# Quarters of x and of two weight chunks multiplied together, and the last norm's work divided anew

## The chip, the cores and the metric

The kernel runs on one core of a Trainium2 chip. The metric is device microseconds of one execution; three runs of the kernel before gave a median of 1205.68 us (1205.36 to 1205.92). Engines are called by the names of the profile: PE (TensorE), DVE (VectorE), ACT (ScalarE), POOL (GpSimd), SP (SyncE, which here only issues transfers).

## What is computed

An encoder trunk of two layers on x of 256 tokens by 1024 channels, all in fp32. Each layer adds half a gated feed-forward, then three token mixers that share one input projection, then half a second feed-forward; a root-mean-square norm closes the trunk. The change touches the first feed-forward of the first layer and the last norm:

```python
def rmsnorm(x, g):
    r = lax.rsqrt(jnp.mean(xf * xf, axis=-1, keepdims=True) + EPS)
    return (xf * r * g.astype(jnp.float32)).astype(x.dtype)

def swiglu(h, w_in, w_out):
    g, u = jnp.split(h @ w_in, 2, axis=-1)
    return (jax.nn.silu(g) * u) @ w_out

x = x + 0.5 * swiglu(rmsnorm(x, norm_ffn1[l]), w_ffn1_in[l], w_ffn1_out[l])   # first step of a layer
...
return rmsnorm(x, norm_final)                                                  # the end
```

## The kernel before

**Precision by halves.** Each fp32 operand is split into a rounded part (hi, made by an ACT cast) and the remainder (lo, a subtraction on DVE, L307), and each product is three PE products: hi with hi, hi with lo, lo with hi (`mm3`, L323 to L325).

**Weights** come in chunks of 1 MB, [128, 8, 256] or [128, 2, 1024], through three raw buffers (`wraw`); `ahead` keeps loads five chunks and splits three chunks in front of their use. SP issues these loads one after the other; a load waits until its buffer is free. In what follows chunk 0 and chunk 1 are the first gate and up chunk of w_ffn1_in, chunk 2 and 3 the next gate and up chunk, and the chunk after 3 is the first of w_ffn1_out.

**The feed-forward** (`ffn`) goes over 11 pairs of gate and up chunks. For a pair, 48 products make the gate sums and 48 the up sums (8 K tiles, 2 halves, 3 products). Norm and projection commute: x is scaled by the norm's gain alone (xgh, xgl), and the factor r of each token is applied after the product, by R, which PE spreads over the partitions from a diagonal dg (L372). Then DVE gr = gate x R (L481), ACT silu (L482), POOL gr x R (L483), DVE hid (L503), ACT hh (L509), POOL hl (L510), and the products with w_out, one pair later (`outp`).

**The start** (L1003 to L1040): x comes as two halves of 128 tokens into a raw buffer; PE runs a few products on ones (`warm`), transposes x (ps_x), ACT and DVE make xgh and xgl of two K tiles at a time, and between them ACT and POOL split chunk 0, loaded in four quarters. xT, the squares of x and the sum sst follow, while PE multiplies chunk 0; chunk 1 is loaded and split whole after that.

**The end**: the last output products (`tokacc`) leave token-major sums for two token tiles (tt), in four quarters q each. `evac_tok` adds them to x on DVE and squares them on ACT; DVE multiplies the low 512 channels (LO) by the gain nf, sums and scales the squares, POOL raises them to -0.5, and both token tiles are scaled at the very end (`scale_out`), LO on ACT and the high half (HI) on DVE.

**Order.** PE's order is the order of the code throughout. Blocks marked BY_HAND also keep ACT's and DVE's instructions of that block in the code's order among themselves; all else on ACT, DVE, POOL and SP is placed by a scheduler at build time, which may put instructions of later code between those of a block.

Of the kernel before, what the change touches and what calls it, by code (L numbers as in the profile page):

```python
# [70 lines left out]
def encoder(ctx: ExitStack, tc: tile.TileContext, a, rope, onehot, out):  # L71
# [210 lines left out]
    specs[0] = ([((slice(None), slice(2 * i, 2 * i + 2)), specs[0][0][0][1][:, 2 * i:2 * i + 2]) for i in range(4)],) + specs[0][1:]  # L282
    raws, parts = [], []

    def ahead(n_raw, n_split):
        while len(raws) < min(n_raw, len(specs)):
# [6 lines left out]
            for _ in split(2):  # L293
                pass

    def split(n, eng=None):

        _, shape = specs[len(parts)]
        raw = raws[len(parts)]
        hi = whi.tile([P] + shape, F32R, tag="hi", name="hi")  # L300
        lo = wlo.tile([P] + shape, F32R, tag="lo", name="lo")
        parts.append((hi, lo))
        n = shape[0] // n
        for i in range(0, shape[0], n):
            h = slice(i, i + n)
            nc.scalar.copy(out=hi[:, h], in_=raw[:, h])  # L306
            (eng or nc.vector).tensor_sub(lo[:, h], raw[:, h], f(hi[:, h]))  # L307
            yield

    used = [0]  # L310
# [102 lines left out]
    BY_HAND = {mybir.EngineType.PE, mybir.EngineType.Activation, mybir.EngineType.DVE}  # L413
    late = []

    def ffn(gnext, final=False):
        accs = [bank(acc, "facc") for _ in range(4)]
        if final:
            fl = [x.rearrange("p a s -> p (a s)") for x in accs]
            accs = [fl[0:2], fl[2:4]]  # L420
            xt = [p4.tile([P, D], F32, tag="t4", name="xt") for _ in range(2)]
            fin = [p4.tile([P, D], F32, tag="t4", name="fin") for _ in range(2)]
            nf = p4.tile([P, D], F32, tag="t4", name="nf")
            ss = [sm.tile([P, 4], F32, name="ss") for _ in range(2)]
# [15 lines left out]
        r_fin = [sm.tile([P, 1], F32, name="r_fin") for _ in range(2)] if final else []  # L440

        def evac_tok(tt, q, ps):

            sl = slice(q * 256, (q + 1) * 256)
            nc.vector.scalar_tensor_tensor(out=fin[tt][:, sl], in0=ps, scalar=0.5, in1=xt[tt][:, sl], op0=ALU.mult, op1=ALU.add)
            nc.scalar.activation(out=t1("junk"), in_=fin[tt][:, sl], func=AF.Square, accum_out=ss[tt][:, q:q + 1])
            if (tt, q) == (0, 2):
                gain_lo(0)
            elif (tt, q) == (1, 1):
                rms(0)  # L450
            elif (tt, q) == (1, 3):
                gain_lo(1)
                rms(1)
                scale_out(0)
                scale_out(1)

        def gain_lo(tt):
            nc.vector.tensor_mul(fin[tt][:, LO], fin[tt][:, LO], nf[:, LO])

        def rms(tt):  # L460
            r = r_fin[tt]
            nc.vector.reduce_sum(out=r, in_=ss[tt], axis=AX.X)
            nc.vector.tensor_scalar(out=r, in0=r, scalar1=1.0 / D, scalar2=EPS, op0=ALU.mult, op1=ALU.add)
            nc.gpsimd.tensor_tensor(out=r, in0=r, in1=mhalf[:, 0:1], op=ALU.pow)

        def scale_out(tt):
            nc.scalar.mul(out=fin[tt][:, LO], in_=fin[tt][:, LO], mul=r_fin[tt])
            nc.vector.scalar_tensor_tensor(out=fin[tt][:, HI], in0=fin[tt][:, HI], scalar=r_fin[tt], in1=nf[:, HI], op0=ALU.mult, op1=ALU.mult)
# [17 lines left out]
        pend = None  # L486
        for j in range(NPAIR):
            w, ps = weights(), bank(wk, "gu")
            if j == 0:
                project_first(ps, w)  # L490
                stats_tok()
            else:
                project(ps, w, 0)
                project(ps, w, 1)
                gr = silu(ps)
            w, pu = weights(), bank(wk, "gu")
            project(pu, w, 0)
            if j == 0:
                stats_bcast()
                gr = silu(ps)  # L500
            project(pu, w, 1)
# [499 lines left out]


    ctx.enter_context(tc.manual_schedule(engines={mybir.EngineType.PE}))  # L1003
    ahead(2, 0)
    with tc.manual_schedule(engines=BY_HAND):

        hot = bank(wk, "hot")

        def warm(n):
            for _ in range(n):  # L1010
                nc.tensor.matmul(hot[:, 0, :P], lhsT=ones, rhs=ones, start=True, stop=True)

        warm(6)
        gains(rows, 2 * KT, 0)
        sst = sm.tile([P, 2], F32, name="sst", bufs=1)
        state["sst1"] = sm.tile([P, 2], F32, name="sst1", bufs=1)
        xps = [bank(acc, "ps_x") for _ in range(4)]
        for tt in range(2):
            for m in range(KT):
                nc.tensor.transpose(xps[m // 2][:, m % 2, cs(tt)], xtok[:, tt, cs(m)], ident)  # L1020
            warm(4)
        first = split(4, nc.gpsimd)
        for b in range(4):
            for i in range(2):
                m = 2 * b + i
                nc.scalar.activation(out=xgh[:, m, :], in_=xps[b][:, i, :], func=AF.Identity, scale=gcol[:, m:m + 1])
            for i in range(2):
                scaled_lo(2 * b + i, 0, xps[b][:, i, :])
            next(first)
        for _ in first:  # L1030
            pass
        for b in range(4):
            nc.vector.tensor_copy(out=xT[:, 2 * b:2 * b + 2, :], in_=xps[b])
        for tt in range(2):
            for i in range(2):
                junk = t2("junk").rearrange("p a s -> p (a s)")
                acc_to = sst if i == 0 else state["sst1"]
                nc.scalar.activation(out=junk, in_=xtok[:, tt, i * 512:(i + 1) * 512], func=AF.Square, accum_out=acc_to[:, tt:tt + 1])
        nc.vector.tensor_add(sst, sst, state["sst1"])
        state["sst"] = sst  # L1040
    for l in range(DEPTH):
        ffn(16 + KT * l)
        mixer(l)
        ffn(KT if l == 0 else None, final=(l == DEPTH - 1))

# [31 lines left out]
```

## Time and profile before

| | |
|---|---|
| median of three runs | 1205.68 us |
| the profiled execution | 1204.95 us, span 1203.2 us |
| PE busy | 1176.7 us, 98% of the span, 9748 products |
| DVE, ACT, POOL busy | 850.5, 678.6, 256.8 us |
| moved by DMA | 218.15 MB, mean 181 GB/s |
| mean granted clock of PE | 0.995 |

The span is the time from the first to the last instruction of the profiled execution. Busy PE means that products follow each other without a gap; a busy share of another engine tells nothing of the end unless PE waits for it. The granted clock is the share of PE's full 2.4 GHz that it was allowed; 0.50 is 1.2 GHz.

### The profile page before, as it was taken

To read this page: it belongs to the slowest core of one execution; us is meant where nothing else is said; L and a number is where in the kernel's file an instruction comes from. 1 tells how busy PE (TensorE), PEld (TensorE's weight loads), DVE (VectorE), ACT (ScalarE), POOL (GpSimd) and SP (SyncE) were. 2 spreads that over 40 slices of the span, in tenths; PEclk is the share of its full clock that TensorE was granted. 3 is DMA by queue.
4 is the path that set the end of the run, shared out by engine and by line. 5 is a ranking of instruction groups with operands and counts; after the bars stand their busy time and mean duration, and the time that the engine had idled before them with its cause. 6 is when DMAs were issued, how large, how long until landed. Compare 5 with 4: busy or idle time off the path is not lost.

```text
span 1203.2 us, 23180 instructions
## 1 busy us (share of the span) xinstructions
PE 1176.7 (98%) x9748; PEld 1150.1 (96%) x9748; DVE 850.5 (71%) x1145; ACT 678.6 (56%) x1117; POOL 256.8 (21%) x188
## 2 busy tenths in 40 slices
PE   8999999999999999999999999999998999999997
PEld 8999999998989999999999999998988999999996
DVE  5766668878887776666685656697787868656664
ACT  6444346579876554444454444466998566443443
POOL 2222224300021032121241212241000302212221
PEclk9999999999999999999999999999999999999999
DMA  7759665453545556565555565545443546565550
GB/s 255 257 179 309 205 209 176 141 175 118 172 136 181 176 180 206 181 206 192 195 175 192 194 207 180 192 158 176 141 162 120 174 141 198 193 203 180 193 192 35
DMA packets 169364, 218.15 MB, mean 181 GB/s; under 512 B 4302, under 2 KB 147200, under 8 KB 169260
## 3 DMA queue, kind: packets, MB, share of 16 engines
q1 hardware_dynamic: 168652, 215.09, 54.5%
q8 instruction: 76, 1.25, 0.4%
q10 hardware_dynamic: 464, 1.06, 0.2%
q0 software_dynamic: 144, 0.52, 0.1%
q14 instruction: 28, 0.23, 0.1%
HBM read 215.59 MB, written 4.22 MB: 183 GB/s over the span
## 4 chain that ended last, share of the span: by engine, by line
PE 75%; ACT 11%; DVE 9%; issue 3%; POOL 1%; DMA 0%; POOLq 0%; ACTq 0%
PE gu L324 13%; PE gu L323 13%; PE gu L325 13%; PE facc L323 5%; PE facc L325 5%; PE facc L324 5%; ACT hi L306 3%; DVE lo L307 3%; PE fm L324 2%; PE fm L323 2%; PE fm L325 2%; ACT e L625 2%; PE facc L407 2%; PE facc L406 2%; PE facc L405 2%
## 5 line engine op out<-in xcount | busy, mean ns | idle before, releaser
L307 DVE TENSOR_TENSOR lo<-raw,hi 128x1024 fp32r<-128x1024 f32 x390 | 539.5, 1397 | 138.2 <-ACT hi L306 137.4
L306 ACT CAST hi<-raw 128x1024 fp32r<-128x1024 f32 (+1 forms) x394 | 404.0, 1044 | 405.7 <-issue 352.8
L325 PE MATMUL gu<-xgh,lo 128*128 128x256 f32 x1408 | 389.4, 277 | 1.6 <-POOL lo L307 0.8
L323 PE MATMUL gu<-xgh,hi 128*128 128x256 f32 x1408 | 390.7, 277 | 0.3 <-ACT hi L306 0.3
L324 PE MATMUL gu<-xgl,hi 128*128 128x256 f32 x1408 | 390.1, 277 | 0.3 <-DVE xgl L338 0.3
L325 PEld LDWEIGHTS gu<-xgh,lo 128*128 128x128 f32 x1408 | 264.5, 188 | 2.2 <-POOL lo L307 1.1
L324 PEld LDWEIGHTS gu<-xgl,hi 128*128 128x128 f32 x1408 | 264.5, 188 | 1.8 <-DVE xgl L338 0.7
L323 PEld LDWEIGHTS gu<-xgh,hi 128*128 128x128 f32 x1408 | 264.3, 188 | 1.8 <-ACT hi L306 1.3
L323 PE MATMUL fm<-xgh,hi 128*128 128x256 f32 x640 | 179.7, 281 | 0.0
L324 PE MATMUL fm<-xgl,hi 128*128 128x256 f32 x640 | 178.8, 279 | 0.0
L325 PE MATMUL fm<-xgh,lo 128*128 128x256 f32 x640 | 178.3, 279 | 0.0
L483 POOL TENSOR_TENSOR gr<-gr,R 128x512 f32<-128x512 f32 x44 | 76.9, 1747 | 365.3 <-ACT gr L482 365.3
L325 PEld LDWEIGHTS fm<-xgh,lo 128*128 128x128 f32 x640 | 121.1, 189 | 0.0
L324 PEld LDWEIGHTS fm<-xgl,hi 128*128 128x128 f32 x640 | 120.4, 188 | 0.8
L323 PEld LDWEIGHTS fm<-xgh,hi 128*128 128x128 f32 x640 | 120.2, 188 | 0.1
L323 PE MATMUL facc<-hh,hi 128*128 128x256 f32 x384 | 106.0, 276 | 0.0
L324 PE MATMUL facc<-hl,hi 128*128 128x256 f32 x384 | 106.0, 276 | 0.0
L325 PE MATMUL facc<-hh,lo 128*128 128x256 f32 x384 | 106.0, 276 | 0.0
L510 POOL TENSOR_TENSOR hl<-hid,hh 128x512 fp32r<-128x512 f32 x35 | 62.5, 1787 | 123.7 <-ACT hh L509 123.7
L481 DVE TENSOR_TENSOR gr<-gu,R 128x512 f32<-128x512 f32 x44 | 30.4, 691 | 74.0 <-PE gu L325 73.8
L324 PEld LDWEIGHTS facc<-hl,hi 128*128 128x128 f32 x384 | 72.1, 188 | 0.0
L323 PEld LDWEIGHTS facc<-hh,hi 128*128 128x128 f32 x384 | 72.1, 188 | 0.0
(234 smaller groups left out, 1949.7 us busy)
## 6 DMA issues: line engine op xcount, KB each, us to landing
raw<-in_w_ffn_in_dram SPq DMA_DIRECT2D x87, 1024.0 KB, 5.1
raw<-in_w_ffn_out_dram SPq DMA_DIRECT2D x44, 1024.0 KB, 4.9
raw<-in_w_in_dram SPq DMA_DIRECT2D x38, 1024.0 KB, 5.1
raw<-in_w_branch_dram SPq DMA_DIRECT2D x12, 1024.0 KB, 5.2
raw<-in_w_out_dram SPq DMA_DIRECT2D x8, 1024.0 KB, 4.9
G<-skew SPq DMA_DIRECT2D x24, 192.0 KB, 5.0
raw<-in_w_in_dram SPq DMA_DIRECT2D x8, 512.0 KB, 4.8
skew<-vec_d SPq DMA_DIRECT2D x6, 512.0 KB, 8.7
```

Source lines behind the costliest of these rows:

```text
L306: nc.scalar.copy(out=hi[:, h], in_=raw[:, h])
L307: (eng or nc.vector).tensor_sub(lo[:, h], raw[:, h], f(hi[:, h]))
L323: nc.tensor.matmul(ps, lhsT=hi[:, k, sl], rhs=xh, start=st, stop=False, **chk)
L324: nc.tensor.matmul(ps, lhsT=hi[:, k, sl], rhs=xl, start=False, stop=False, **chk)
L325: nc.tensor.matmul(ps, lhsT=lo[:, k, sl], rhs=xh, start=False, stop=last, **chk)
L405: nc.tensor.matmul(ps, lhsT=xh[:, k, cs(tt)], rhs=w[0][:, k, sl], start=(first and k == 0), stop=False)
L406: nc.tensor.matmul(ps, lhsT=xh[:, k, cs(tt)], rhs=w[1][:, k, sl], start=False, stop=False)
L407: nc.tensor.matmul(ps, lhsT=xl[:, k, cs(tt)], rhs=w[0][:, k, sl], start=False, stop=(last and k == 1))
L481: nc.vector.tensor_mul(gr, ps, Rb)
L483: nc.gpsimd.tensor_mul(gr, gr, Rb)
L510: nc.gpsimd.tensor_sub(hl, hid, f(hh))
L625: nc.scalar.activation(out=e[:, qt, :], in_=e[:, qt, :], func=AF.Identity, scale=su[:, qt:qt + 1])
```

## The change

x goes into two [128, 2, 512] tiles of another pool and comes in four quarters of 256 channels (two K tiles) each, for all 256 tokens. Chunks 0 and 1 come in quarters of two K tiles too, the three kinds in turn, two of the quarters on ACT's queue and the rest on SP's. For each quarter PE transposes its two K tiles, ACT and DVE make xgh and xgl, and split the quarter of chunk 0 and of chunk 1 (DVE takes the lo of chunk 0 that POOL made); PE multiplies the quarter with chunk 0, transposes the next quarter, and multiplies with chunk 1. The first pair thus enters `ffn` as `begun`, and its R, silu and hid follow in the middle of chunk 2. ACT loads its table early, by an activation on mhalf. In the last norm nf is scaled once by sqrt(D); the LO product moves from DVE to POOL, the squares of a tile's last quarter from ACT to DVE, the sums become single additions, and each token tile is scaled and stored as soon as its own sums are there.

The diff, cut to its core:

```diff
+    xtok = [p4.tile([P, 2, D // 2], F32, tag="t4", name="xtok") for _ in range(2)]
+    raws = [wraw.tile([P, KT, 2 * P], F32, tag="raw", name="raw") for _ in range(2)]
+    for q in range(4):
+        nc.sync.dma_start(out=xtok[q // 2][:, :, 256 * (q % 2):256 * (q % 2 + 1)], in_=xv[:, :, 256 * q:256 * (q + 1)])
+        for i, raw in enumerate(raws):
+            src = a["w_ffn1_in"][0, 256 * q:256 * (q + 1), i * D_FF:i * D_FF + 2 * P]
+            (nc.scalar if i == 0 and q < 2 else nc.sync).dma_start(out=raw[:, 2 * q:2 * q + 2, :], in_=src.rearrange("(k p) n -> p k n", p=P))
...
-            nc.scalar.activation(out=t1("junk"), in_=fin[tt][:, sl], func=AF.Square, accum_out=ss[tt][:, q:q + 1])
-            if (tt, q) == (0, 2):
-                gain_lo(0)
...
-                scale_out(1)
+            if q < 3:
+                nc.scalar.activation(out=t1("junk"), in_=fin[tt][:, sl], func=AF.Square, accum_out=ss[tt][:, q:q + 1])
+            else:
+                nc.vector.tensor_tensor_reduce(out=t1("junk"), in0=fin[tt][:, sl], in1=fin[tt][:, sl], scale=1.0, scalar=ss[tt][:, 0:1], op0=ALU.mult, op1=ALU.add, accum_out=ss[tt][:, 3:4])
+                rms(tt)
+            if q == 1:
+                nc.gpsimd.tensor_mul(fin[tt][:, LO], fin[tt][:, LO], nf[:, LO])
+                nc.vector.tensor_scalar(out=ss[tt][:, 0:1], in0=ss[tt][:, 0:1], scalar1=ss[tt][:, 1:2], scalar2=EPS * D, op0=ALU.add, op1=ALU.add)
...
+                project(ps, w, 0)
+                if begun:
+                    stats_bcast()
+                    pend = hidden(0, begun[1], silu(begun[0]))
+                    begun = None
+                project(ps, w, 1)
...
+        splits = [split(4) for _ in range(2)]
         for b in range(4):
...
+            for c in range(2):
+                next(splits[c])
+                for m in (2 * b, 2 * b + 1):
+                    for t in range(2):
+                        mm3(begun[c][:, t, :], parts[c], m, cs(t), xgh[:, m, :], xgl[:, m, :], False, m == KT - 1, start=(m == 0 and t == 0))
+                if c == 0 and b < 3:
+                    turn(b + 1)
```

The scheduler's part of the change shows in the order of the instructions. ACT's queue at the start, in the kernel before; raw_139 is chunk 0, raw_144 chunk 1, raw_232 chunk 2, and hi_192, hi_238, hi_244 are their rounded parts:

```order
L1026 ACTIVATE xgh_129<-ps_x_160,gcol_131 128x256
L306 CAST hi_192<-raw_139 128x512 [waits DMAHW3_49]
L1026 ACTIVATE xgh_129<-ps_x_161,gcol_131 128x256 [waits PE_49]
L1026 ACTIVATE xgh_129<-ps_x_161,gcol_131 128x256
L306 CAST hi_192<-raw_139 128x512 [waits DMAHW4_49]
```

And now, where raw_105 is chunk 0, raw_106 chunk 1 and raw_363 chunk 2:

```order
L1044 ACTIVATE xgh_142<-ps_x_155,gcol_144 128x256
L309 CAST hi_189<-raw_105 128x512 [waits DMAHW2_49]
L309 CAST hi_209<-raw_106 128x512 [waits DMAHW3_49]
L309 CAST hi_373<-raw_363 128x1024 [waits DMAHW5_49]
L309 CAST hi_373<-raw_363 128x1024
L1044 ACTIVATE xgh_142<-ps_x_156,gcol_144 128x256 [waits PE_49]
L1044 ACTIVATE xgh_142<-ps_x_156,gcol_144 128x256
L309 CAST hi_189<-raw_105 128x512 [waits DMAHW4_49]
L309 CAST hi_209<-raw_106 128x512 [waits DMAHW6_49]
```

Both casts of chunk 2, which stood behind all of chunk 0, chunk 1 and the squares, now stand between quarter 0 and quarter 1; DVE's two subtractions for chunk 2 stand at the same place in its queue. SP's load of chunk 2 stands behind all the quarters of x and of chunks 0 and 1.

DVE's queue behind the last quarter, now (before, the copies of xT stood ahead of the sum sst):

```order
L1064 TENSOR_TENSOR sst_329<-sst_329,sst1_330 128x2 [waits Activation_49]
L1066 COPY xT_141<-ps_x_155 128x512
L1066 COPY xT_141<-ps_x_156 128x512
L1066 COPY xT_141<-ps_x_157 128x512
L1066 COPY xT_141<-ps_x_158 128x512
L358 TENSOR_SCALAR v_tok_349<-sst_329 128x2 [waits DVE_49]
L310 TENSOR_TENSOR lo_380<-raw_365,hi_379 128x1024 [waits DMAHW1_49,PE_49,Activation_49]
L362 TENSOR_SCALAR dg_353<-ident_96,r_tok_350 128x128 [waits Pool_49]
```

The copies of xT have moved between the sum and v, and so ahead of dg.

DVE's queue at the end, now; fin_12111 is token tile 0, fin_12112 token tile 1 (before, the scaling of both tiles' HI half stood last):

```order
L449 SCALAR_TENSOR_TENSOR fin_12111<-facc_12106,xt_12109 128x256
L453 ISA junk_13858,ss_12114<-fin_12111,ss_12114 128x256 [waits DVE_49]
L453 ISA ss_12114 128x1
L462 TENSOR_TENSOR ss_12114<-ss_12114 128x1 [waits DVE_49,Activation_49]
L465 SCALAR_TENSOR_TENSOR fin_12111<-fin_12111,ss_12114,nf_12113 128x512 [waits Pool_49]
L449 SCALAR_TENSOR_TENSOR fin_12112<-facc_12107,xt_12110 128x256 [waits PE_49]
```

Tile 0's scaling, which waits for POOL, now stands ahead of tile 1's first evacuation. On POOL the order is tile 0's LO product, tile 0's power, tile 1's LO product, tile 1's power.

## Rows read from the trace of the kernel before

**Rows 1.** Busy times by stage: stretch, length, busy time (count) by engine, clock, DMA, GB/s.

```profile
9.45:10.50 1.05, 0.58 (x4) 0.58 (x5) 0.72 (x2) 1.05 (x4) 1.05 (x2) 1.00 1.09 345
20.00:25.00 5.00, 5.00 (x42) 4.84 (x41) 3.07 (x4) 3.19 (x4) 0.00 (x0) 1.00 0.82 297
1198.00:1199.00 1.00, 0.00 (x0) 0.00 (x0) 0.55 (x2) 0.44 (x1) 0.53 (x1) 1.00 0.42 156
1199.00:1200.00 1.00, 0.00 (x0) 0.00 (x0) 0.31 (x1) 0.28 (x1) 0.00 (x0) 0.50 0.98 367
```

**Rows 2.** Timeline of PE: start, duration, engine, line, operation, tiles, count, idle before.

```profile
1.05 2.93 PE L1011 MATMUL hot<-ones 128*128 128x128 f32 x12 [1.05 <-DVE ind L143]
5.42 1.06 PE L1011 MATMUL hot<-ones 128*128 128x128 f32 x8
6.70 1.09 PE L1020 MATMUL ps_x<-ident,xtok 128*128 128x128 f32 x8 [0.22 <-DMA xtok<-in_x_dram]
19.59 0.59 PE L372 MATMUL halves<-dg,ones 128*128 128x256 f32 x2
22.85 0.28 PE L323 MATMUL gu<-xgh,hi 128*128 128x256 f32 x1
34.35 0.28 PE L323 MATMUL facc<-hp,hi 128*128 128x256 f32 x1
```

**Rows 3.** Timeline of ACT at the start.

```profile
8.41 0.85 ACT L1026 ACTIVATE xgh<-ps_x,gcol 128x256 fp32r<-128x256 f32 x2
9.13 0.63 ACT L306 CAST hi<-raw 128x512 fp32r<-128x512 f32 x1
20.82 2.00 ACT L306 CAST hi<-raw 128x1024 fp32r<-128x1024 f32 x2 [4.22 <-DMA raw<-in_w_ffn_in_dram]
25.83 1.28 ACT L482 ACT_TABLE_LOAD   x1
27.12 0.63 ACT L482 ACTIVATE gr<-gr 128x512 f32<-128x512 f32 x1
```

**Rows 4.** The chain that ended last, at ACT's squares of x: start, duration, piece.

```profile
12.27 2.45 ACT junk L1038 x8
```

**Rows 5.** Timeline of DVE at the start.

```profile
9.29 0.87 DVE L338 SCALAR_TENSOR_TENSOR xgl<-ps_x,gcol,xgh 128x256 fp32r<-128x256 f32 x2 [0.37 <-ACT xgh L1026]
12.59 2.47 DVE L1033 COPY xT<-ps_x 128x512 f32<-128x512 f32 x4
15.69 2.36 DVE L307 TENSOR_TENSOR lo<-raw,hi 128x1024 fp32r<-128x1024 f32 x2 [0.36 <-ACT hi L306]
17.97 0.48 DVE L359 TENSOR_SCALAR dg<-ident,r_tok 128x128 f32<-128x128 f32 x2
24.18 0.42 DVE L374 COPY R<-halves 128x256 f32<-128x256 f32 x1
24.63 0.69 DVE L481 TENSOR_TENSOR gr<-gu,R 128x512 f32<-128x512 f32 x1
```

**Rows 6.** DMA issues of the first 4 us: tensor, queue, count, size, median us to landing.

```profile
raw<-in_w_ffn_in_dram SPq DMA_DIRECT2D x1, 1024.0 KB, 8.4
```

**Rows 7.** Timeline of SP's queue at the start: issue of chunk 0's quarters and chunk 1.

```profile
1.19 2.81 SPq L290 DMA_DIRECT2D raw<-in_w_ffn_in_dram  x5
```

**Rows 8.** Timeline of POOL at the start.

```profile
15.41 0.71 POOL L356 TENSOR_TENSOR r_tok<-v_tok,mhalf 128x2 f32<-128x2 f32 x1 [1.76 <-DVE v_tok L355]
27.83 1.30 POOL L483 TENSOR_TENSOR gr<-gr,R 128x512 f32<-128x512 f32 x1 [11.71 <-ACT gr L482]
```

**Rows 9.** Timeline of ACT, POOL and DVE in the last 12 us.

```profile
1192.71 0.19 ACT L446 ACTIVATION_READ_ACCUMULATOR junk<-fin 128x1 f32 x1
1195.36 0.55 POOL L464 TENSOR_TENSOR r_fin<-r_fin,mhalf 128x1 f32<-128x1 f32 x1 [7.92 <-DVE r_fin L463]
1197.53 0.99 POOL L464 TENSOR_TENSOR r_fin<-r_fin,mhalf 128x1 f32<-128x1 f32 x1 [1.62 <-DVE r_fin L463]
1198.56 0.75 DVE L468 SCALAR_TENSOR_TENSOR fin<-fin,r_fin,nf 128x512 f32<-128x512 f32 x1 [0.45 <-POOL r_fin L464]
```

More of the change, by code (lines that the diff above doesn't have):

```diff
@@ L280, in encoder @@
         specs += ffn_chunks(a["w_ffn2_in"][l], a["w_ffn2_out"][l])
-    specs[0] = ([((slice(None), slice(2 * i, 2 * i + 2)), specs[0][0][0][1][:, 2 * i:2 * i + 2]) for i in range(4)],) + specs[0][1:]
-    raws, parts = [], []
+    parts = []
     def ahead(n_raw, n_split):
@@ L294, in ahead, with split @@
                 pass
-    def split(n, eng=None):
+    def split(n):
         _, shape = specs[len(parts)]
@@ L306, in split @@
             nc.scalar.copy(out=hi[:, h], in_=raw[:, h])
-            (eng or nc.vector).tensor_sub(lo[:, h], raw[:, h], f(hi[:, h]))
+            nc.vector.tensor_sub(lo[:, h], raw[:, h], f(hi[:, h]))
             yield
@@ L414, in encoder, with ffn @@
     late = []
-    def ffn(gnext, final=False):
+    def ffn(gnext, final=False, begun=None):
         accs = [bank(acc, "facc") for _ in range(4)]
@@ L425, in ffn @@
             nc.gpsimd.dma_start(out=nf, in_=a["norm_final"].partition_broadcast(P))
+            nc.gpsimd.tensor_scalar_mul(nf, nf, math.sqrt(D))
         def back(tt):
@@ L439, in ffn @@
         LO, HI = slice(0, 512), slice(512, 1024)
-        r_fin = [sm.tile([P, 1], F32, name="r_fin") for _ in range(2)] if final else []
         def evac_tok(tt, q, ps):
@@ L445, in evac_tok @@
             nc.vector.scalar_tensor_tensor(out=fin[tt][:, sl], in0=ps, scalar=0.5, in1=xt[tt][:, sl], op0=ALU.mult, op1=ALU.add)
[L446 to L458 removed]
+            if q < 3:
[6 more added lines that the diff above has]
+                nc.vector.tensor_scalar(out=ss[tt][:, 0:1], in0=ss[tt][:, 0:1], scalar1=ss[tt][:, 1:2], scalar2=EPS * D, op0=ALU.add, op1=ALU.add)
         def rms(tt):
[L461 to L463 removed]
+            r = ss[tt][:, 3:4]
+            nc.vector.tensor_tensor(out=r, in0=r, in1=ss[tt][:, 2:3], op=ALU.add)
             nc.gpsimd.tensor_tensor(out=r, in0=r, in1=mhalf[:, 0:1], op=ALU.pow)
[L466 to L468 removed]
+            nc.scalar.mul(out=fin[tt][:, LO], in_=fin[tt][:, LO], mul=r)
+            nc.vector.scalar_tensor_tensor(out=fin[tt][:, HI], in0=fin[tt][:, HI], scalar=r, in1=nf[:, HI], op0=ALU.mult, op1=ALU.mult)
             for sl, eng in ((LO, nc.scalar), (HI, nc.sync)):
@@ L484, in silu, with hidden @@
             return gr
[L486 to L501, printed above, removed]
+        def hidden(j, pu, gr):
             hid = t2("hid")
@@ L510, in ffn, with loads @@
             nc.gpsimd.tensor_sub(hl, hid, f(hh))
+            return j, hh, hl
+        def loads(j):
+            if j == len(late):
+                late.append(load_late(j))
+        pend = None
+        if begun:
+            stats_tok()
+            loads(0)
+        for j in range(1 if begun else 0, NPAIR):
+            w, ps = weights(), bank(wk, "gu")
+            if j == 0:
+                project_first(ps, w)
+                stats_tok()
+            else:
+                project(ps, w, 0)
+                if begun:
+                    stats_bcast()
+                    pend = hidden(0, begun[1], silu(begun[0]))
+                    begun = None
+                project(ps, w, 1)
+                gr = silu(ps)
+            w, pu = weights(), bank(wk, "gu")
+            project(pu, w, 0)
+            if j == 0:
+                stats_bcast()
+                gr = silu(ps)
+            project(pu, w, 1)
+            here = hidden(j, pu, gr)
             if pend:
                 outp(*pend)
-            pend = (j, hh, hl)
+            pend = here
             if final and 2 <= j < 4:
                 back(j - 2)
-            if j == len(late):
-                late.append(load_late(j))
+            loads(j)
         if final:
@@ L1003, in encoder, with turn @@
     ctx.enter_context(tc.manual_schedule(engines={mybir.EngineType.PE}))
-    ahead(2, 0)
     with tc.manual_schedule(engines=BY_HAND):
-        hot = bank(wk, "hot")
+        hot = half()
         def warm(n):
             for _ in range(n):
-                nc.tensor.matmul(hot[:, 0, :P], lhsT=ones, rhs=ones, start=True, stop=True)
+                nc.tensor.matmul(hot[:, :P], lhsT=ones, rhs=ones, start=True, stop=True)
+        xps = [bank(acc, "ps_x") for _ in range(4)]
+        def turn(b):
+            for tt in range(2):
+                for i in range(2):
+                    c = 2 * (b % 2) + i
+                    nc.tensor.transpose(xps[b][:, i, cs(tt)], xtok[b // 2][:, tt, cs(c)], ident)
+        nc.scalar.activation(out=mhalf, in_=mhalf, func=AF.Identity)
         warm(6)
         gains(rows, 2 * KT, 0)
[L1015 to L1022, printed above, removed]
+        warm(4)
+        turn(0)
+        warm(6)
+        begun = [bank(wk, "gu") for _ in range(2)]
+        used[0] = 2
+        splits = [split(4) for _ in range(2)]
         for b in range(4):
@@ L1028, in encoder @@
                 scaled_lo(2 * b + i, 0, xps[b][:, i, :])
[L1029 to L1033, printed above, removed]
+            for c in range(2):
[5 more added lines that the diff above has]
+                    turn(b + 1)
+        for s in splits:
+            for _ in s:
+                pass
+        sst = sm.tile([P, 2], F32, name="sst", bufs=1)
+        state["sst1"] = sm.tile([P, 2], F32, name="sst1", bufs=1)
         for tt in range(2):
@@ L1037, in encoder @@
                 acc_to = sst if i == 0 else state["sst1"]
-                nc.scalar.activation(out=junk, in_=xtok[:, tt, i * 512:(i + 1) * 512], func=AF.Square, accum_out=acc_to[:, tt:tt + 1])
+                nc.scalar.activation(out=junk, in_=xtok[i][:, tt, :], func=AF.Square, accum_out=acc_to[:, tt:tt + 1])
         nc.vector.tensor_add(sst, sst, state["sst1"])
+        for b in range(4):
+            nc.vector.tensor_copy(out=xT[:, 2 * b:2 * b + 2, :], in_=xps[b])
         state["sst"] = sst
     for l in range(DEPTH):
-        ffn(16 + KT * l)
+        ffn(16 + KT * l, begun=begun)
+        begun = None
         mixer(l)
```

3 lines of the change are left out of this document (removed).

## The prediction

> **What bounds the kernel now.** I read the busy table by stage first. TensorE (PE) is busy for all of 20 to 25 us, with 42 products in 5.00 us, one per 0.119 us [rows 1], and so it goes nearly to the end: the kernel is a chain of PE products, so a delay at its head is carried to its end, and only the head and the tail offer gains. For the head I read the timelines of PE, ACT, DVE and POOL and the DMA view, for the tail the last 12 us of the same. The timelines show a second thing: each engine takes its instructions strictly in order. ACT stood 4.22 us before a cast whose load had not landed, and DVE copied R at 24.18 though its source was ready by 20.18 (19.59 + 0.59), because two lo subtractions stood ahead of it [rows 2, 3, 5]. So what matters is not only which work the change adds but what stands in front of what. Fixed points of before: chunk 1 is done and chunk 2's products begin at 22.85, the first output product starts at 34.35 [rows 2].
>
> **The head: one hoisted pair of casts.** The listing shows that ACT, after its share of quarter 0, now casts chunk 2 whole (2 instructions) before it scales quarter 1 of x; DVE has chunk 2's two subtractions at the same place. Behind these four queue quarters 1 to 3 of x, of chunk 0 and of chunk 1, and so PE. The first question is when chunk 2 lands (L).
>
> - *L.* Before, chunk 1 was the fifth load of SP's five (issued in 2.81 us from 1.19, so at about 3.4) and took 8.4 us: it landed near 11.8 [rows 6, 7]. By then x, chunks 0 and 1 and 0.26 MB of rope had come, 3.4 MB. Now chunk 2 stands behind x, chunk 0 and chunk 1 on the same queue: 4.2 MB, 0.8 MB more, at the 345 GB/s of that stretch [rows 1] 2.3 us: 14.1, and I take 14.3. Ends: 13.4 at a faster flow, 14.9 if rope still mixes in. ACT and DVE reach the pair near 8.4 and stand for some 6 us.
> - *Quarter 1 after L.* ACT: two casts 2.00, two scalings 0.85, the cast of a quarter 0.53 (0.63 with its end) [rows 3]: L+3.4. DVE: lo of chunk 2, second half, L+3.4 (1.18 each, half of 2.36); two xgl 0.87, L+4.3; a lo of 128x512, half of a 1.18, 0.62: L+4.95 [rows 5]. PE runs freely from L+5.0.
> - *The quarters.* One turn of the loop: 12 products of chunk 0 (two done early, 1.2), four transposes 0.55 (half of 1.09 [rows 2]), then scalings 0.85, cast 0.53, lo 0.62 and hand-overs 0.05, while the 12 products of chunk 1 hide in those 2.05: 3.8. Two turns and a last 2.6: L+15.2.
> - *The clock.* PE idles from about 11.7 to L+3.4. In the tail the granted clock fell from 1.00 to 0.50, that is from 2.4 to 1.2 GHz, after PE's last products, between 1198 and 1200 [rows 1]; so I take it to fall in this gap too. At the lower level 12 products took 2.93 us at the start, later ones 8 in 1.06: 0.244 against 0.133 [rows 2]. Until it rises, 1.2 us of products and 0.55 of transposes run about twice as long: +1.7. The quarters end at L+16.9 = 31.2, against 22.85: **+8.35**. If the clock stays up, 1.7 less.
>
> The extra DVE work (lo of chunk 0, which POOL did) is in these numbers. The early ACT table load costs nothing: ACT waits for x then.
>
> **After the quarters.** Call T the last transposes' end: L+16.9 less 4.6 (2.05 front, 1.2, 1.35) = L+12.3 = 26.6. ACT: scalings and two casts to T+1.9, squares 2.45 [rows 4] to T+4.4. DVE now adds the squares *before* copying xT (2.47) and forms v *after*: T+7.1; v and POOL's power, 0.71 [rows 8], to T+8.1; a lo of chunk 3 in between ends T+8.45; dg 0.48 [rows 5]: T+8.95. PE needs dg at T+7.45 (24 x 0.119 after T+4.6): wait 1.5. Second half of chunk 2: T+12.05. DVE: three lo 3.55, R 0.42, gr 0.69 [rows 5]: T+13.65, and chunk 3 needs the bank that gr reads: wait 1.6. Then table load 1.28, silu 0.63 [rows 3], POOL 1.30 [rows 8], hid 0.69 (as gr), hh 0.63 (as silu), and POOL's hl, 1.30 by the same row, with a few hand-overs: T+19.9, while PE is there at T+19.35: wait 0.5. Output products start at T+19.9 = 46.5 against 34.35: **+12.1**. The first 8.35 is part of it; the rest are these three waits, none of which before has. Loads of chunk 3 on find their buffers late too, but land ahead of these times (chunk 3's buffer frees at L+3.4). Ends: +7.5 (clock up, early L, half the waits) and +14.
>
> In this sum L rests on loads that land in the order of issue, as chunk 1, issued last, landed last in 8.4 us. The Trainium skill, "DMA: Bandwidth & Descriptors", section "Queues, rings and completion order", says that descriptors are taken in ring order but that completion is not FIFO per issuing engine. If that let chunk 2 overtake the quarters, rival 1 would hold; no run here shows such an overtaking.
>
> **The tail.** The change takes two multiplications by nf and two sums off DVE, and puts nf's low half on POOL, the last quarter's squares on DVE, and token tile 0's HI scaling on DVE in front of tile 1's evacuations. That scaling waits for POOL's power, which waits for POOL's product. In order: ACT's second sum ends 1192.90 [rows 9]; POOL's product to 1194.25 (1.30 as its 128x512 gr product [rows 8]; the two powers took 0.55 and 0.99 [rows 9], so POOL's work can stretch by 1.8 beside DVE, and I stretch half of it for the upper end); DVE meanwhile two evacuations, squares (each about half of 0.87), and the sum, to 1194.6; power 0.55: 1195.2; HI(0) 0.75: 1195.95. Only now tile 1's first evacuations, which wait for no other engine but PE: 1196.7; ACT's squares, after its own LO(0), 1197.25; POOL's product 1198.55; DVE's last two evacuations, squares and sum 1198.9; power to 1199.5. Before, HI(1) began at 1198.56 [rows 9]: **+1.0**; I take +1.2, ends +0.6 and +2.1. The transfers behind it keep their length: before, the last ones also went alone. Scaling nf by 32 on POOL in the mixer hides, as POOL is idle there; cost 0, at worst one late ybl under PE's other branch products.
>
> Sum: 1204.95 (the profiled execution) + 12.1 + 1.2 = 1218.25; the median stands 0.7 above that execution: **1219**.
>
> **Rivals.**
> 1. *Chunk 2 lands early and holds nobody.* Then L is ACT's own arrival, 8.4, the clock stays up, quarters end at 8.4 + 15.2 = 23.6, T = 19.0, output products at 38.9, +4.55; with +1.2 and 0.7: **1211.4**. For it: the queue's descriptors are spread over 16 engines. Against: 3.1 MB stand ahead of chunk 2, and 3.1 MB by 8.4 us was never near.
> 2. *Faster.* As rival 1, and the hand-overs hide too: PE paces the quarters. Ready for quarter 0 at 8.1, four times 24 x 0.119 plus three times 0.55: 21.2, 1.65 sooner than 22.85, no wait for dg, gr or hl; in the tail POOL's product takes no time that DVE waits for, so that DVE's saved product with nf shows (0.69, as gr of the same size): 1204.95 - 1.65 - 0.69 + 0.7 = **1203.3**. For it: in the rest of the kernel PE alone sets the pace, and quarters let it start on two chunks at once. It decides if all of x and both chunks are split within 2.9 us per quarter and chunk 2 lies on its buffer by 8.4. Against: ACT and DVE need 2.05 us between transposes and products, more than the 1.43 that chunk 1 covers.
> 3. *Deeper.* The prefetch, once late, runs dry again: the first output chunk can load only when chunk 0's buffer is free (T+2) and the next chunk only after it. For it: half a load uncovered (a load moves 1.05 MB at 345 GB/s in 3 us, and needs its issue and landing besides): **1221** and above. Against: ACT casts it at T+7, PE wants it at T+19.
>
> **How the numbers follow.** Forecast 0.74 (two in three of it with the fallen clock, else near 1217.3), rival 1 0.13, rival 2 0.06, rival 3 0.07. A measurement of this kernel tells 0.2%, 2.4 us, from no change. Rival 2 lies just at that bound below: faster 0.05; same 0.04; slower 0.91. The range takes the forecast's ends (+7.5 + 0.6 gives 1213.7; +14 + 2.1 gives 1221.8) and half of rival 1's neighbourhood: 1211 to 1222.
>
> **What would show it.** Right: in the new trace ACT's first cast of 128x1024 starts near 14.3 after a wait of about 6 us on a load; PE has a gap of 5 to 8 us after 24 products, then a granted clock of 0.50; the R product starts 1 to 2 us after PE could take it; output products start near 46; in the tail DVE stands for POOL before tile 1's first evacuation. Wrong: that cast runs before 10 us, or PE works through to 23 us, or 1206 or less.

## The result and the profile after

The changed kernel took 1221.65 us, median of four runs (1221.18 to 1222.32); the kernel before, run on the same chip beside it, 1205.52 us (1204.21 to 1205.92). The ratio is 1.0134, with a 95% interval of 1.0122 to 1.0147: 16 us slower. The profiled execution took 1222.32 us, its span is 1220.4 us, 17.2 more than the span before.

Where these 17.2 us lie, read from three fixed points of both traces: the first output product started at 48.12 us where it had started at 34.35 [rows 2], **+13.8 in the head**; from there to PE's last product it took 1.7 us more; and from there to the end of the span another 1.7.

**The head.** ACT's timeline at the start, kernel after (start, duration, engine, line, operation, tiles, count, idle before and what ended it); it answers to [rows 3]:

```profile
6.48 1.13 ACT L309 CAST hi<-raw 128x512 fp32r<-128x512 f32 x2
16.20 1.99 ACT L309 CAST hi<-raw 128x1024 fp32r<-128x1024 f32 x2 [8.58 <-DMA raw<-in_w_ffn_in_dram]
18.09 0.83 ACT L1044 ACTIVATE xgh<-ps_x,gcol 128x256 fp32r<-128x256 f32 x2
...
24.46 0.84 ACT L1044 ACTIVATE xgh<-ps_x,gcol 128x256 fp32r<-128x256 f32 x2 [4.52 <-PE ps_x L1029]
...
28.77 0.84 ACT L1044 ACTIVATE xgh<-ps_x,gcol 128x256 fp32r<-128x256 f32 x2 [2.44 <-PE ps_x L1029]
```

ACT had split quarter 0 by 7.6 us. Then it stood 8.58 us before the cast of chunk 2, in front of the scaling of quarter 1 of x, whose four transposes had ended at 10.0 (0.60 from 9.41). PE in the same stretch; it answers to [rows 2]:

```profile
19.48 0.58 PE L326 MATMUL gu<-xgh,hi 128*128 128x256 f32 x1 [8.09 <-ACT hi L309]
...
21.07 0.58 PE L328 MATMUL gu<-xgh,lo 128*128 128x256 f32 x1 [0.41 <-DVE lo L310]
...
21.45 0.42 PE L326 MATMUL gu<-xgh,hi 128*128 128x256 f32 x1
...
23.37 1.05 PE L1029 MATMUL ps_x<-ident,xtok 128*128 128x128 f32 x4
...
31.17 0.38 PE L328 MATMUL gu<-xgh,lo 128*128 128x256 f32 x1 [0.50 <-DVE lo L310]
...
33.86 0.28 PE L326 MATMUL gu<-xgh,hi 128*128 128x256 f32 x1
...
38.02 0.70 PE L375 MATMUL halves<-dg,ones 128*128 128x256 f32 x2 [1.17 <-DVE dg L362]
...
42.58 0.36 PE L326 MATMUL gu<-xgh,hi 128*128 128x256 f32 x1 [1.12 <-DVE gr L478]
...
48.12 0.28 PE L326 MATMUL facc<-hp,hi 128*128 128x256 f32 x1
```

PE stood 8.09 us for the quarter's cast, ran slowly to 24 us, was paced by the hand-overs of each turn (0.50 before the lo product), and later waited for dg and for gr. The 24 products ahead of the wait for dg are the first half of chunk 2: they began at 33.86, against 22.85 before. The clock, by two-microsecond stretches (stretch, length, busy time and count of PE, PEld, DVE, ACT, POOL, granted clock, DMA share, GB/s):

```profile
12.00:14.00 2.00, 0.00 (x0) 0.00 (x0) 0.00 (x0) 0.00 (x0) 0.00 (x0) 1.00 1.10 349
14.00:16.00 2.00, 0.00 (x0) 0.00 (x0) 0.00 (x0) 0.00 (x0) 0.00 (x0) 0.58 0.81 253
16.00:18.00 2.00, 0.00 (x0) 0.00 (x0) 0.73 (x1) 1.80 (x2) 0.00 (x0) 0.50 0.01 3
...
24.00:26.00 2.00, 2.00 (x16) 1.88 (x15) 0.66 (x2) 1.53 (x4) 0.00 (x0) 0.86 0.09 27
26.00:28.00 2.00, 1.51 (x11) 1.30 (x12) 1.41 (x3) 0.33 (x1) 0.00 (x0) 1.00 0.00 0
```

With nothing on PE the granted clock went from 2.4 to 1.2 GHz (1.00 to 0.50), and PE's products from 19.48 to 24 us ran at that level before it rose. The DMA column shows the other half: the loads ran at 349 GB/s while three engines stood still, until the last of chunk 2 was in. The first 16 us of the DMA view, in 40 slices of 0.4 us, 4.47 MB in all, and under it the same slices of the kernel before:

```profile
GB/s 0 0 0 0 23 156 270 296 210 317 333 295 251 325 351 333 292 369 374 384 374 374 384 356 351 351 348 348 353 343 351 346 348 348 353 347 355 302 209 53
```

```profile
GB/s 0 0 0 0 113 83 245 369 379 392 420 407 397 389 361 366 358 346 361 369 361 356 358 343 351 346 355 365 269 101 6 0 0 0 0 0 56 82 187 287
```

**The tail.** DVE and POOL in the timeline of the kernel after; PE's last product ended at 1211.09. It answers to [rows 9]:

```profile
1208.45 1.29 POOL L456 TENSOR_TENSOR fin<-fin,nf 128x512 f32<-128x512 f32 x1 [5.53 <-ACT junk L451]
...
1210.38 0.55 POOL L463 TENSOR_TENSOR ss<-ss,mhalf 128x1 f32<-128x1 f32 x1 [0.63 <-DVE ss L462]
...
1210.96 0.75 DVE L465 SCALAR_TENSOR_TENSOR fin<-fin,ss,nf 128x512 f32<-128x512 f32 x1 [0.66 <-POOL ss L463]
...
1211.63 0.74 DVE L449 SCALAR_TENSOR_TENSOR fin<-facc,xt 128x256 f32<-128x256 f32 x2
...
1213.99 0.68 DVE L453 CUSTOM_DVE_ANT_0 junk<-fin,ss 128x256 f32<-128x256 f32 x1
...
1215.61 0.75 DVE L465 SCALAR_TENSOR_TENSOR fin<-fin,ss,nf 128x512 f32<-128x512 f32 x1 [0.67 <-POOL ss L463]
```

Tile 0's scaling stands for POOL's power, and tile 1's first evacuation, the row at 1211.63, comes behind it. Tile 1's HI scaling started 4.52 us after PE's end; before it was 2.95 (1198.56 [rows 9] less 1195.61, where PE's last product, 0.40 long from 1195.21, ended).

### The profile page after: what moved, and what is told of

It is laid out like the page before. It is cut to its first block, busy times and chain, and to the rows that moved or that the text cites. A ratio compares the mean times of both kernels' runs of the same rounds, so it can differ in the third digit from the quotient of the medians.

```text
span 1220.4 us, 23198 instructions
## 1 busy us (share of the span) xinstructions
PE 1182.1 (97%) x9752; PEld 1154.5 (95%) x9752; DVE 853.4 (70%) x1153; ACT 678.3 (56%) x1116; POOL 258.6 (21%) x187
## 4 chain that ended last, share of the span: by engine, by line
PE 72%; ACT 11%; DVE 9%; issue 3%; POOL 2%; POOLq 0%; ACTq 0%; DVEq 0%
PE gu L327 13%; PE gu L326 13%; PE gu L328 12%; PE facc L326 5%; PE facc L327 5%; PE facc L328 5%; DVE lo L310 3%; ACT hi L309 3%; PE fm L327 2%; PE fm L326 2%; PE fm L328 2%; ACT e L636 2%; PE facc L410 2%; PE br L327 2%; PE facc L409 2%
## 5 line engine op out<-in xcount | busy, mean ns | idle before, releaser
L310 DVE TENSOR_TENSOR lo<-raw,hi 128x1024 fp32r<-128x1024 f32 (+1 forms) x396 | 542.2, 1383 | 143.3 <-ACT hi L309 142.8
L328 PEld LDWEIGHTS facc<-hh,lo 128*128 128x128 f32 x384 | 72.1, 188 | 0.0
```

Of the source, the lines that this page charges most:

```text
L310: nc.vector.tensor_sub(lo[:, h], raw[:, h], f(hi[:, h]))
L328: nc.tensor.matmul(ps, lhsT=lo[:, k, sl], rhs=xh, start=False, stop=last, **chk)
```

## The experiments

Three points of each trace say what it did: when chunk 2's first product started (for a kernel whose dg waits, 24 x 0.119 us and the wait back from R's product), when the first output product started, and the time.

**Only the place of the pair (e1, e5).** The scheduler had put chunk 2's split between quarter 0 and quarter 1. Here it is written by hand, behind quarter 3 (e1) or behind quarter 1 (e5):

```diff
         for s in splits:
             for _ in s:
                 pass
+        ahead(3, 3)          # e1
...
                 if c == 0 and b < 3:
                     turn(b + 1)
+            if b == 1:
+                ahead(3, 3)  # e5
```

> The changed kernel, with chunk 2's two casts (and its two subtractions on DVE) written by hand behind the four quarters, so that the scheduler cannot put them between quarter 0 and quarter 1. Theory A (the hoisted pair holds the quarters): ACT's 128x1024 cast still waits for nothing but the quarters, PE has no gap of 8 us after 24 products, the clock stays at 1.00, the quarters end near 23 to 24 instead of 32, the wait for dg grows to 3 to 4 us since chunk 2's split now stands ahead of the squares, output products start near 41 instead of 48, and the time is 1214 to 1216 us (6 to 8 below the changed kernel). Theory B (the loads or the hand-overs of four quarters set the pace, the pair only filled the time): quarters end at 30 or later, time 1220 or more.

> The changed kernel with chunk 2's two casts and subtractions written by hand behind quarter 1 instead of behind quarter 0 where the scheduler put them. Theory A (what counts is the number of quarters queued behind the pair): the pair still starts when chunk 2 lands, 16 us, but one turn of the loop (4.3 us in the changed kernel, from 24.46 to 28.77) now stands ahead of it; the quarters end some 4 us sooner, output products start near 44, time 1217 to 1218.5. Theory B (the pair's place does not matter, loads or hand-overs do): 1220.5 or more.

Measured: e1 1213.84 us (1.0082 of the kernel before, 1.0066 to 1.0098), e5 1216.74 (1.0099, 1.0085 to 1.0113), both a little under theory A's ranges; chunk 2's first product at 24.85 and 28.76 instead of 33.86, the first output product at 42.78 and 43.25 instead of 48.12. So of the 16 us, 7.8 by the medians or 6.3 by the ratios (1.0134 and 1.0082) go by moving four instructions, and the number of quarters behind them counts: that is theory A of both, though in e1 the clock did not stay at 1.00 as A had it. ACT's timeline of e1, and under it R's product in PE's timeline of e1 and of e5:

```profile
11.18 0.84 ACT L1044 ACTIVATE xgh<-ps_x,gcol 128x256 fp32r<-128x256 f32 x2 [2.46 <-PE ps_x L1029]
...
15.47 0.84 ACT L1044 ACTIVATE xgh<-ps_x,gcol 128x256 fp32r<-128x256 f32 x2 [2.43 <-PE ps_x L1029]
```

```profile
30.96 1.22 PE L375 MATMUL halves<-dg,ones 128*128 128x256 f32 x2 [3.26 <-DVE dg L362]
```

```profile
32.96 0.70 PE L375 MATMUL halves<-dg,ones 128*128 128x256 f32 x2 [1.35 <-DVE dg L362]
```

Two things stand in them. A turn of the loop takes 4.29 us with the clock up, of which ACT waits 2.4 for PE: nothing of the next quarter is ready while PE multiplies this one. And with the quarters sooner by 9.0 the output products came only 5.3 sooner. In e1 dg stood not only behind squares and xT: chunk 2's two casts (1.99) now stood ahead of the squares, and PE waited 3.26 for it, against 1.17 in the changed kernel and 1.35 in e5, where the casts stand ahead of quarter 2. In and after e1's gap the clock was down again (the columns are those of the stretches above):

```profile
28.00:30.00 2.00, 0.00 (x0) 0.00 (x0) 1.81 (x4) 1.98 (x3) 1.16 (x1) 1.00 0.75 178
30.00:36.00 6.00, 5.04 (x21) 4.86 (x22) 3.31 (x6) 3.12 (x4) 1.66 (x2) 0.53 1.05 372
```

The traced execution of e1 is the slowest of its four (1217.69 us; the others 1212.33 to 1214.75), so how long the clock was down there, and the 42.78, need not hold for the others.

**Only the clock (e2, e6).** Products on ones after quarter 0 keep PE at work while it would wait:

```diff
                 if c == 0 and b < 3:
                     turn(b + 1)
+            if b == 0:
+                warm(58)   # e2; e6: warm(30)
```

> The changed kernel with 58 products on ones (128x128, 0.125 us each) put on PE after quarter 0, so that PE works for some 7 of the 8.1 us in which it waited for the hoisted casts. Nothing else differs. Theory A (the idle gap costs the clock and the low clock costs 1.7 us): the granted clock stays at 1.00 through 14 to 26 us, the 12 products behind the gap take 0.12 each instead of 0.21, output products start near 46.5 instead of 48.1, time 1.5 to 1.9 below the changed kernel, 1220. Theory B (ACT and DVE set the end of the quarters whatever PE's clock is): the clock is high but output products start within 0.4 of 48.1.

> The changed kernel with 30 products on ones on PE after quarter 0. In the run with 58 they were recorded as 116 products and took 13.1 us, so that PE came back at 24.5, 5 us too late; 30 should take 6.8 us, from 11.3 to 18.1, and end before the pair is through at 19.4. Theory A (the idle gap lets the clock fall and that costs 1.5 to 1.7 us): granted clock 1.00 from 10 to 28 us, output products start near 46.5 instead of 48.1, time 1.5 to 1.9 below the changed kernel, 1220. Theory B (ACT and DVE set the pace of the quarters whatever PE's clock is): clock 1.00 and output products within 0.4 of 48.1.

e2 was too large a dose, and both its theories missed: 1223.28 us. A product on ones is recorded as two, so PE came back at 24.53, 5 us late; the clock stayed at 1.00. e6 has the right one; PE's timeline:

```profile
12.58 6.86 PE L1021 MATMUL halves<-ones 128*128 128x128 f32 x60
...
20.68 0.38 PE L328 MATMUL gu<-xgh,lo 128*128 128x256 f32 x1 [0.60 <-DVE lo L310]
...
46.45 0.28 PE L326 MATMUL facc<-hp,hi 128*128 128x256 f32 x1
```

Its clock was 1.00 throughout the head, the lo product of quarter 1 took 0.38 instead of 0.58, and the first output product started 1.67 us sooner than in the changed kernel; 1219.52 us, 2.1 below it, or 1.8 by the two ratios. Not all of the 1.67 is the clock, for chunk 2 also came 0.40 sooner, as ACT's timeline shows (16.20 in the changed kernel):

```profile
15.80 1.99 ACT L309 CAST hi<-raw 128x1024 fp32r<-128x1024 f32 x2 [6.86 <-DMA raw<-in_w_ffn_in_dram]
```

From this cast to the first output product it took 30.65 us in e6, and 31.92, 31.92 and 31.95 in the three traces of the changed kernel (two of them e12 and e13 below). So the fallen clock cost 1.27 to 1.30 us in the head. Of e2 a useful rest remains: although PE came back 5.05 us later than in the changed kernel, its output products started only 2.34 later (50.46), since by then all of quarter 1 was made and the clock was up.

**What led to R, into the gaps (e7); transposes first (e8).** e7 has chunk 2's and chunk 3's split by hand behind the quarters, squares of x on ACT after quarters 1 and 3, an xT copy on DVE after each quarter's lo, and dg behind chunk 2's lo alone. e8 is e7 with one more move: the transposes of the next quarter stand ahead of the products of this one.

```diff
         for b in range(4):
+            if b < 3:
+                turn(b + 1)       # e8
...
-                if c == 0 and b < 3:
-                    turn(b + 1)   # e8
+            if b < 3:
+                nc.vector.tensor_copy(out=xT[:, 2 * b:2 * b + 2, :], in_=xps[b])
+            if b % 2:
+                for tt in range(2):
...
+                    nc.scalar.activation(out=junk, in_=xtok[b // 2][:, tt, :], func=AF.Square, accum_out=(sst if b == 1 else state["sst1"])[:, tt:tt + 1])
...
+        nc.gpsimd.tensor_tensor(out=r, in0=v, in1=mhalf[:, 0:2], op=ALU.pow)
+        nc.vector.tensor_copy(out=xT[:, 6:8, :], in_=xps[3])
+        ahead(3, 3)
+        for tt in range(2):
+            nc.vector.tensor_scalar_mul(dg[:, cs(tt)], ident, r[:, tt:tt + 1])
+        ahead(4, 4)
```

> The changed kernel with chunk 2's and chunk 3's splits by hand behind the quarters, and the work that led to R put into the gaps of the quarters: squares of x on ACT after quarters 1 and 3, each xT copy on DVE after its quarter's lo, then sum, v, power, chunk 2's lo, dg. PE's order is that of the changed kernel. Theory A (with the pair moved, 24.9 is where the quarters end and the rest of the head's loss is dg behind xT and squares): no wait for dg (3.26 with the pair alone moved), no clock dip near 30 us, output products 11.5 us after chunk 2's first product as in the kernel before, so at 36 to 37, time 1208.5 to 1210. Theory B (with one wait gone the next one, for chunk 3's split, gr's bank or hl, ends as late): output products at 39 or later, 1211 and above.

> As the kernel with the work in the gaps, and each quarter's transposes stand ahead of the products of the quarter before, so that ACT and DVE make the next quarter while PE multiplies this one. Theory A (a turn of 4.3 us is PE's 1.85 between transposes in series with ACT's and DVE's 2.4; side by side PE's 24 x 0.119 + 0.55 = 3.4 sets it): the quarters end 2.7 to 3.6 sooner, chunk 2's first product near 21.5, output products near 33, time 1204.5 to 1206 with the new tail (about +1.7). Theory B (the loads set the pace, or PE stands for a quarter of x that has not landed): chunk 2's first product at 23 or later, 1207 and above.

e7: 1210.02 us (1.0041, 1.0027 to 1.0054), at the upper edge of what theory A gave (the first output product, at 37.10, is 0.1 past it). R's product no longer waits, and the output products start 12.45 us after chunk 2's first product (24.65), with 0.73 for gr's bank left; PE's timeline:

```profile
27.50 0.60 PE L375 MATMUL halves<-dg,ones 128*128 128x256 f32 x2
...
31.57 0.36 PE L326 MATMUL gu<-xgh,hi 128*128 128x256 f32 x1 [0.73 <-DVE gr L478]
...
37.10 0.28 PE L326 MATMUL facc<-hp,hi 128*128 128x256 f32 x1
```

e8: 1205.71 us (1.0004, 0.9995 to 1.0013): chunk 2's first product at 20.94, output products at 33.86, half a microsecond before the kernel before. PE's timeline, and one row of ACT's:

```profile
11.97 0.60 PE L1028 MATMUL ps_x<-ident,xtok 128*128 128x128 f32 x4
...
15.16 0.60 PE L1028 MATMUL ps_x<-ident,xtok 128*128 128x128 f32 x4
...
33.86 0.28 PE L326 MATMUL facc<-hp,hi 128*128 128x256 f32 x1
```

```profile
15.80 0.84 ACT L1047 ACTIVATE xgh<-ps_x,gcol 128x256 fp32r<-128x256 f32 x2 [1.32 <-PE ps_x L1028]
```

Turns now come 3.19 us apart, which is PE's own work of 24 products and four transposes (3.4 by the rows of before), and ACT waits 1.32 in a turn without squares where it waited 2.4. So the head of quarters, rightly ordered, is no loss.

**The tail (e3, e9, e11).** e3 is the kernel before with the new last norm alone; e9 is e8 with the old one. e11 is e8 with the new one, but both token tiles scaled behind tile 1's sum:

```diff
             nc.gpsimd.tensor_tensor(out=r, in0=r, in1=mhalf[:, 0:1], op=ALU.pow)
+            if tt == 1:
+                scale_out(0)
+                scale_out(1)
+
+        def scale_out(tt):
+            r = ss[tt][:, 3:4]
             nc.scalar.mul(out=fin[tt][:, LO], in_=fin[tt][:, LO], mul=r)
```

> The kernel before, with the new last norm alone (LO product on POOL, last quarter's squares and single additions on DVE, each token tile scaled as soon as its sums are there; nf scaled on POOL); the start is that of before. Theory A (DVE's wait for POOL ahead of tile 1's first evacuation lengthens the tail): tile 1's HI scaling starts 4.5 us after PE's end instead of 2.95, time 1.4 to 1.8 above the kernel before, 1207.2. Theory B (the tail is a gain and the whole loss is in the head): 0.5 to 0.9 below the kernel before.

> The kernel with transposes first, with the last norm of the kernel before. Theory A (the tail's loss of 1.7 adds to the head's whatever the head does): 1.5 to 2.0 below the run with the new tail, 1202.5 to 1204, 0.1 to 0.2% under the kernel before. Theory B (head and tail do not add, or the head's gain is lost in the middle): not below the kernel before.

> The kernel with transposes first and the new tail, where token tile 0 is scaled and stored only after tile 1's sum, as the kernel before did; POOL keeps the LO product, DVE the last quarter's squares and the single additions. Theory A (the tail's loss is DVE's stand for POOL ahead of tile 1's first evacuation): that evacuation starts within 0.4 us of PE's end, tile 1's HI scaling 2.6 to 3.1 us after PE's end instead of 4.9, time 1.6 to 2.2 below the run with the new tail, so within 0.4 of the run with the old tail. Theory B (the loss is the slower work itself: squares of 0.68 on DVE and a product of 1.29 on POOL): HI scaling at 3.8 or later, time less than 1 us below.

e3: 1206.87 us against 1204.85 (1.0019, 1.0011 to 1.0028), 2.0 above and a little more than theory A's 1.4 to 1.8; e9: 1203.41 (0.9989, 0.9980 to 0.9997), 2.3 below e8, or 1.8 by the two ratios, as theory A had it; e11: 1204.38 (0.9988, 0.9978 to 0.9998), 1.3 below e8, or 1.9 by the two ratios. Tile 1's HI scaling started 4.52 us after PE's end in e3 and in e8 (e11's expectation says 4.9), 2.94 in e9, 3.49 in e11, whose timeline reads:

```profile
1194.60 0.75 DVE L449 SCALAR_TENSOR_TENSOR fin<-facc,xt 128x256 f32<-128x256 f32 x2
...
1195.07 0.40 PE L410 MATMUL facc<-hi,hl 128*128 128x512 f32 x1
...
1195.99 0.21 DVE L457 TENSOR_SCALAR ss<-ss 128x1 f32<-128x1 f32 x1 [0.65 <-ACT junk L451]
...
1196.12 0.75 DVE L449 SCALAR_TENSOR_TENSOR fin<-facc,xt 128x256 f32<-128x256 f32 x2
...
1197.93 0.99 POOL L463 TENSOR_TENSOR ss<-ss,mhalf 128x1 f32<-128x1 f32 x1 [0.63 <-DVE ss L462]
...
1198.96 0.75 DVE L471 SCALAR_TENSOR_TENSOR fin<-fin,ss,nf 128x512 f32<-128x512 f32 x1 [0.45 <-POOL ss L463]
```

Theory A holds for two thirds; its 2.6 to 3.1 for the HI scaling was missed, and so was B's 3.8. Without the stand for POOL, tile 1's first evacuations start before PE's end and 1.03 of the 1.58 us are gone. The other 0.55 is a second, smaller stand of the same kind, which A did not have: the added sum at 1195.99 waits 0.65 for ACT's squares, and the last two evacuations, which need only PE, come behind it. This part is read from the rows; no run took that stand away.

e9 and e11 are the two versions of this study that end below the kernel before, by 0.1%. With the interval's end at 0.9997 and 0.9998, that is about as little as these runs can tell.

**The middle (e12, e13, e14).** The changed kernel twice more and the kernel before once more, for the 1.7 us that the trace has between head and tail. In the first layer's mixer PE waits some 3 us for one result of DVE in both kernels (2.98 and 3.00), and the clock goes down. Stretches of before, under them of after, and under these one of e13:

```profile
338.00:340.00 2.00, 0.63 (x3) 0.63 (x4) 1.96 (x4) 1.98 (x4) 0.00 (x0) 0.71 0.00 0
340.00:342.00 2.00, 2.00 (x11) 2.00 (x11) 1.76 (x7) 1.93 (x4) 0.00 (x0) 0.50 0.19 25
342.00:344.00 2.00, 2.00 (x18) 2.00 (x18) 2.00 (x6) 1.99 (x5) 0.00 (x0) 0.94 1.02 337
```

```profile
354.00:356.00 2.00, 2.00 (x11) 2.00 (x11) 1.77 (x7) 1.93 (x4) 0.00 (x0) 0.50 0.27 41
356.00:358.00 2.00, 2.00 (x12) 2.00 (x11) 2.00 (x7) 1.99 (x6) 0.00 (x0) 0.50 1.06 369
358.00:360.00 2.00, 2.00 (x15) 2.00 (x15) 2.00 (x5) 1.18 (x5) 1.56 (x1) 0.73 0.59 205
```

```profile
354.00:356.00 2.00, 2.00 (x20) 2.00 (x19) 1.76 (x8) 1.93 (x4) 0.00 (x0) 1.00 0.32 71
```

> The changed kernel once more, for its stretches of low clock and the landing of chunk 2. Theory A (the low stretch in the first layer's mixer, 6.8 us instead of 3.4, is not the change's doing; in the runs so far 3.4 or 6.8 appeared in either mixer, whatever the head was): 3.4 or 6.8 at 350 to 360, and the cast of chunk 2 starts at 15.5 to 16.3. Theory B (the shifted head lengthens it): 6.8 there in both looks.

> The changed kernel a third time. Theory A: 3.4 or 6.8 at 350 to 360, so that of three looks not all show 6.8. Theory B: 6.8 in all three.

> The kernel before once more. Theory A: a low stretch of 3.4 or 6.8 in either mixer near 338 and 928, by chance. Theory B (only a shifted head makes 6.8): 3.4 in both.

Summed over such stretches, the low level at the first layer's mixer lasted 6.8 us in the first trace of the changed kernel and 3.4 in the second (e12, 1221.17 us); the third (e13, 1219.32 us) had none there, which neither theory gave. In e14 it was 3.4 in both mixers, as in the first trace of the kernel before, which both theories allow. 3.4 us more at half the clock can cost up to 1.7 us, which is as much as the middle had grown by. Elsewhere 6.8 appeared in e8 there, and in e1, e3 and e5 in the second layer's mixer; e3 has the start of the kernel before. So a shifted head does not make it 6.8, and theory B fails: the length differs from execution to execution of one kernel. In the first mixer 6.8 came only under heads of quarters (the changed kernel and e8, against 3.4 in the three traces with the old start); whether the change makes it more frequent, so few traces do not tell.

## Why the prediction was right, and by how much its terms were off

It said slower, at 1219, and for the reason that the runs confirm; the time is 2.7 us higher, near the upper end of the range. By its steps:

- *L*, 14.3 predicted, **16.2** measured (15.56 to 16.22 in the six traces where ACT stood for it), outside its ends. The sum counted 4.2 MB up to L and left out rope's 0.26 MB, which shares the stretch: 4.47 MB by 16 us, and 0.75 us at 345 GB/s. The flow also began more slowly than before: by 11.6 us 3.13 MB had come where 3.38 had (the two DMA rows above), 0.74 us at the same rate. And it ran out slowly, at 302, 209 and 53 GB/s in its last 1.2 us, some 0.55 more. Together that is about the 2.1 from the sum's 14.1. It is read, not shown: no run left rope out, and why the flow began slowly stays open. In all six traces the cast starts only as the flow runs out; no load was seen to overtake, which the Trainium skill, "DMA: Bandwidth & Descriptors", section "Queues, rings and completion order", would allow. That was the condition of rival 1, and it fell with it.
- *PE free at L+5.0*: 21.07 is L+4.87.
- *The turns*, 3.8 each: **4.3** in e1 and in the changed kernel. The path goes over DVE's two xgl (0.88) and lo (0.64), as the sum itself had it for quarter 1, and not over ACT's cast (0.53); for two turns 1.0 too little.
- *The clock*, +1.7 if it falls: it fell, and cost 1.27 to 1.30 by e6, so the term was 0.4 too large. It rested on a row that does not show it: the 12 products in 2.93 us at the start [rows 2] were taken for the lower level, but the trace of the kernel before has a granted 1.00 there, and why they were slow stays open:

```profile
2.00:3.00 1.00, 1.00 (x7) 1.00 (x6) 0.00 (x0) 0.00 (x0) 0.00 (x0) 1.00 0.58 194
```

  At a granted 0.50 the changed kernel's products of quarter 1 came 0.21 us apart and four transposes took 1.05; at 1.00, in e6, it was 0.12 and 0.60.
- *Quarters' end*: 33.86 against 31.2, so 2.7 late, by L and the turns less what the clock's term had too much.
- *The three waits*: 1.17 for dg (1.5 predicted), 1.12 for gr's bank (1.6), none for hl (0.5). ACT's table load had gone ahead, at 38.16, while ACT waited for gr: my sum had it on the path. Together 1.3 less. Output products: 48.12 against 46.5. So part of the closeness is luck: L and the turns were 2.9 too short, the clock and the waits 1.7 too long. That e1's wait for dg was longer (3.26) does not speak against the term: there two casts stood ahead of the squares, which is not so in the changed kernel.
- *The tail*, +1.2 predicted: 1.57 at the HI scaling, 1.7 to the end of the span, inside its ends. The mechanism is the one named; mis-sized were DVE's squares, 0.71 and 0.08 for the sum's read-out where half of 0.87 stood, and left out was DVE's stand for ACT's second sum.
- *Left out*: the clock in the middle's mixers. It can move a single execution by over a microsecond either way; the sum was made against one in which both stretches were 3.4 us.
- *Rival 2* (a head that PE paces) had the right mechanism for another kernel: e8 put the transposes first and came to 20.94 against its 21.2. Its condition, that ACT and DVE make a quarter beside PE's products, failed in the changed kernel since the transposes stood in the middle of them, as its "against" said. *Rival 3* did not come: ACT's casts of the first output chunk waited 1.18 for its load, to 36.15, but PE never stood for them.

## What to carry to other kernels

A step that splits work into pieces is worth nothing until the queues have been read in the order in which they will run: here one pair of casts for the next chunk, put by the scheduler between two pieces, cost 6.3 us, what stood ahead of dg 4.9, one line of transposes in the middle of the products 4.5, and the tail 1.8. These are the steps from the changed kernel over e1, e7 and e8 to e9 by their ratios, each known to some 2 us; another order of the steps might share them out otherwise. With all of them undone 1.3 us are left as a gain. In an in-order queue, ask of every instruction that waits for another engine or a load what stands behind it that does not; that holds for the prefetch, for xT ahead of dg, and for a scaling ahead of an evacuation alike. When such a stand opens a gap in PE, add the clock to its price, and read it from a run with the gap filled, counted from the event that ended the wait, since that event moves too.

## What was not expected of the hardware

The same PE gap of some 3 us (2.98 to 3.29) in the first layer's mixer was followed by 0, 3.4 or 6.8 us at 1.2 GHz in three executions of one kernel, which can be a good part of their spread (1219.32 to 1222.32 us). And POOL's power took 0.71 or 1.54 us for 128x2, and 0.55 or 0.99 for 128x1; in the rows read here the longer ones (1.54 at 35.91 in the changed kernel, 0.99 at 1197.93 in e11) ran beside DVE work between SBUF tiles (a lo subtraction, a scaling), those of 0.55 while DVE stood or evacuated PSUM. The 0.71 at 15.41 [rows 8] does not fit well, as a lo subtraction ran beside more than half of it too [rows 5]. No run was made to tell that cause from others.
